# A float32 trunk whose weights are split in two parts: two rings of twelve slots instead of six tiles, wider operations, and one more seven-product row pair per block

## Chip, cores and metric

The kernel runs on one core of one Trainium2 chip. The metric is the device time of one execution in microseconds; the time before is the median of three runs. The lines of the profile come from one further execution, taken by the hardware profiler.

## The reference

A trunk of two layers works on 256 tokens of width 2048 (float32). Each layer has a token mixer (layer 0: HGRN2, layer 1: gated linear attention), a four-head attention into 256 memory tokens, an output projection, and a SwiGLU FFN. The change touches above all the FFN:

```python
hn = _rmsnorm(h, norm_ffn[layer])
gate, up = jnp.split(hn @ w_gate_up[layer], 2, axis=-1)
h = h + (jax.nn.silu(gate) * up) @ w_down[layer]
```

`w_gate_up` is 2048 x 11264 and `w_down` 5632 x 2048; the projections of the mixers (`hn @ w_in`), of the memory (`mem_n @ w_kv`) and of the output (`@ w_out`) use the same machinery for their weights.

## The kernel before

**Numbers in two parts.** TensorE multiplies in the rounded type fp32r. To keep float32 precision every operand is written as a high part (the value rounded to fp32r) and a low part (the rest), and a product is three matmuls: high x high, high x low, low x high (lines 249 to 251 in `project`, 333 to 335 in `product`). The activations are split once. The weights stream from HBM into "raw" tiles of 4 x 512 columns (four of them, line 199) and are split by `split` (line 201): ScalarE copies up to 1024 columns into the high half of a "parts" tile (line 207), and VectorE subtracts that from the raw weights into the low half (line 208). There are six parts tiles, each with two slots of 512 columns in both parts; a new one waits until TensorE has read the tile six before it.

**Plain projections.** `weights` (line 212) loads four row tiles of up to 512 columns in one transfer and splits them in two calls; `project` (line 220) multiplies them for both token halves. The FFN's down step, `w_out`, `w_in` and `w_mem_kv` go this way.

**Gate and up.** The FFN works through 11 blocks of 512 gate columns and the 512 up columns that belong to them (`up_block`, line 823). In a block, `project_halves` (line 321) goes over 8 row pairs; a pair is a 2 x 2 product of blocks (two token halves, two row tiles, gate and up). It is done in one of three ways, by a letter in `KINDS` (line 818):

- "S": seven products instead of eight, in Winograd's manner. VectorE first forms combinations of the weights in place in the raw tile, with 1024, 512 and 512 columns (lines 350 to 352); three of the four original weights and four combinations are split, in calls of 512, 1024, 1024 and 1024 columns (lines 346, 347, 353, 354).
- "O": eight products from the four original weights, two splits of 1024.
- "H": eight products too, for a pair whose activations were prepared for "S"; one combination of 512 columns (line 366) and a split of it more.

`PAIRS` (line 267) says for which kind the activations of each pair are prepared. After the eight pairs a block adds its seven sums together (lines 828 to 835), then come two down steps (`down`, line 842) on blocks that are done, each with up to two quads of four row tiles and two token halves. The work of each engine is written in program order; the order that the engines really get is fixed at build time by a scheduler that may take a later step first where an earlier one is not ready. On the chip each engine keeps to that order.

**Kinds per block:** block 0 "SHOSHOSO", blocks 1 and 2 "SHOSSOSO", blocks 3 to 10 "SSOSSOSS".

**Other tiles in the parts buffers.** The attention's keys and values for the memory (line 436) and the gate weights of layer 1 (lines 766 to 773) lie in tiles of the same six (`side`, line 193). Those of layer 1 are put away in HBM by one transfer (line 462) and fetched by one (line 767).

Of the kernel before, what the change touches and what calls it, by code (L numbers as in the profile page):

```python
# [9 lines left out]
F32 = mybir.dt.float32  # L10
F32R = mybir.dt.float32r
# [3 lines left out]
ALU = mybir.AluOpType  # L15
AX = mybir.AxisListType

P = 128
T = 256
NT = T // P  # L20
# [4 lines left out]
XA = 512  # L25
XH = 4
DFF = 5632
GR = 16
DK = 192
# [6 lines left out]
def trunk_kernel(ctx: ExitStack, tc: tile.TileContext, x, mem, norm_mix, norm_ffn, norm_mem,  # L36
                 norm_final, hgrn_w_in, hgrn_lb_logits, hgrn_onorm, gla_w_in, gla_w_gk,
                 gla_b_gk, gla_onorm, w_mem_kv, w_out, w_gate_up, w_down, c_ident, c_mask, out):
    nc = tc.nc

    const = ctx.enter_context(tc.tile_pool(name="const", bufs=1))
    wts = ctx.enter_context(tc.tile_pool(name="wts", bufs=1))
# [28 lines left out]
    h = const.tile([P, NT, D], F32, name="h")  # L71
# [106 lines left out]
    def later(*pieces):  # L178
        pending.extend(pieces)
# [12 lines left out]

    def side(shape, name):
        return wts.tile(shape, F32, tag="parts", name=name, bufs=6)

    def new_raw():
# [3 lines left out]

    def split(src, name, by=2):

        n, m = src.shape[1:]
        both = wts.tile([P, 2, 2, 512], F32R, tag="parts", name=f"parts{name}", bufs=6)
        for k in range(0, n, by):
            j = min(k + by, n)
            nc.scalar.copy(out=both[:, 0, k:j, 0:m], in_=src[:, k:j, :])  # L207
            nc.vector.tensor_tensor(out=both[:, 1, k:j, 0:m], in0=src[:, k:j, :],  # L208
                                    in1=both[:, 0, k:j, 0:m].bitcast(F32), op=ALU.subtract)
        return [(both[:, 0, k, 0:m], both[:, 1, k, 0:m]) for k in range(n)]  # L210
# [55 lines left out]

    PAIRS = "SSOSSOSB"
    HOMES = (("hq", "hq"),) * 4 + (("F", "K"), ("T", "sc"), ("Q", None), ("v", "gate"))
# [52 lines left out]
    def project_halves(forms, kinds, w, c0, c1, name):  # L321
# [15 lines left out]
        for p, kind in enumerate(kinds):  # L337
            i, raw = new_raw()

            for j, c in ((slice(0, 4, 3), c0), (slice(1, 3), c1)):  # L340
                nc.sync.dma_start(out=raw[:, j, :],
                                  in_=w[2 * p * P:(2 * p + 2) * P, c:c + 512].rearrange("(k p) c -> p k c", p=P))
            x = forms[p].get
            last = p == len(PAIRS) - 1
            if kind == "S":
                tt = nc.vector.tensor_tensor
                b00, = split(raw[:, 0:1, :], f"{i}a")
                b11, b10 = split(raw[:, 2:4, :], f"{i}b")

                tt(out=raw[:, 0:2, :], in0=raw[:, 0:4:2, :], in1=raw[:, 1:2, :].broadcast_to([P, 2, 512]), op=ALU.subtract)  # L350
                tt(out=raw[:, 2, :], in0=raw[:, 2, :], in1=raw[:, 0, :], op=ALU.add)  # L351
                tt(out=raw[:, 3, :], in0=raw[:, 3, :], in1=raw[:, 2, :], op=ALU.subtract)  # L352
                t5, t7 = split(raw[:, 0:2, :], f"{i}c")
                t6, t4 = split(raw[:, 2:4, :], f"{i}d")
                todo = {1: ("x00", b00), 2: ("x01", b10), 3: ("z", b11), 4: ("x11", t4), 5: ("s", t5), 6: ("u", t6),
                        7: ("d0", t7)}
                for b in (1, 2, 6, 7, 5, 4, 3) if last else (1, 3, 2, 5, 7, 6, 4):
                    product(b, x(todo[b][0]), todo[b][1])
            else:
                b00, b01 = split(raw[:, 0:2, :], f"{i}a")  # L360
                b11, b10 = split(raw[:, 2:4, :], f"{i}b")
                todo = [[(2, "x00", b00), (5, "x10", b01), (4, "x10", b00), (3, "d0", b01)]]
                if kind == "O":
                    todo.append([(2, "x01", b10), (5, "x11", b11), (4, "x11", b10), (3, "d1", b11)])
                else:
                    nc.vector.tensor_tensor(out=raw[:, 3, :], in0=raw[:, 3, :], in1=raw[:, 2, :], op=ALU.subtract)
                    e1, = split(raw[:, 3:4, :], f"{i}c")
# [67 lines left out]
    for l in range(2):  # L435
        kv = side([P, 2, XH * T], f"kv{l}")
        kT.append(kv[:, 0, :].rearrange("p (h t) -> p h t", t=T))
        vm.append(kv[:, 1, :].rearrange("p (m c) -> p m c", c=XA))
        ps = project(memq, range(NQ), w_mem_kv[l], 0, XA, f"mk{l}", prep=prep_mem if l == 0 else None)
# [20 lines left out]

    kv_out = away.tile([P, 2, XH * T], F32, name="kv_out")
    later(lambda: nc.scalar.dma_start(out=kv_out, in_=kv))


    def attention(l, ps, r, yq):
# [35 lines left out]
        def turn_probs(m):  # L501
            pT = st["pT", m] = work.tile([P, XH, T], F32, tag=("T", "sc")[m], name=f"pT{l}{m}")
# [260 lines left out]
    def gla(hq, r, yq):  # L763
        w = gla_w_in[0]
        half = (GR + XA) // 2
        kv = side([P, 2, XH * T], "kv")
        nc.scalar.dma_start(out=kv, in_=kv_out)
        kT[1] = kv[:, 0, :].rearrange("p (h t) -> p h t", t=T)
        vm[1] = kv[:, 1, :].rearrange("p (m c) -> p m c", c=XA)
        gk = side([P, 6, T], "gk")  # L770
        wgk = gk[:, 0:4, :]
        nc.gpsimd.memset(wgk, 0.0)
        nc.sync.dma_start(out=wgk[0:GR, :, 0:DK], in_=gla_w_gk[0].rearrange("r (h c) -> r h c", c=DK))
        psx = [project(hq, range(NQ), w, 3 * MIX + i * half, half, f"gx{i}") for i in range(2)]
        low = gk[:, 4, :].rearrange("p (t c) -> p t c", c=P)
# [3 lines left out]
        lowT = gk[:, 5, :]  # L779
        dec = {}  # L780
# [5 lines left out]
        def decay(pr):  # L786
# [3 lines left out]
            for a in range(2):  # L790
                hd = 2 * pr + a
                zp = aux_ps(f"zp{hd}")
                for j in range(2):
                    nc.tensor.matmul(zp[:, j * T:(j + 1) * T], wgk[:, hd, j * P:(j + 1) * P], lowT,
                                     start=True, stop=True)
# [21 lines left out]

    KINDS = ("SHOSHOSO", "SHOSSOSO", "SHOSSOSO", "SSOSSOSS")

# [136 lines left out]
```

## Time and profile before

| | |
|---|---|
| median of 3 runs | 2327.83 us (2327.59 to 2328.57) |
| profiled execution, its own time | 2328.0 us |
| its span, first to last instruction | 2326.2 us |
| granted TensorE clock | 0.999 |
| matmuls and transposes on TensorE | 11034 |
| split subtracts (line 208) of 1024 columns | 374, 1220 ns each |
| split copies (line 207) of 1024 columns | 374, 1050 ns each |
| data moved | 435.51 MB, 187 GB/s |

In the profile PE is TensorE's matmul, PEld its weight load, DVE VectorE, ACT ScalarE, POOL GpSimd, SP the engine whose queue issues most loads. A timeline row gives start and duration in us, engine, line, operation, output and input with their shapes, and, in brackets, how long the engine was idle before it and what released it. Names like "parts163c" are the third split of raw tile 163. Busy time of TensorE is a weak sign of how full it is, since a matmul's 0.39 us overlap with the next one; the distance between starts tells more, and the same holds for VectorE.

### The profile page before, as it was taken

Reading aid. Unit: us, or ns where it says so; the run is one execution under the profiler, and the core shown is the slowest. Engines: PE = TensorE matmul, PEld = TensorE weight load, DVE = VectorE, ACT = ScalarE, POOL = GpSimd, SP = SyncE. Lnnn points to the kernel's source line nnn. Section 1 sums busy time; section 2 is a strip of 40 time slices with the busy share of each in tenths; the row PEclk is TensorE's granted clock in tenths of the full one; section 3 lists DMA queues with packets and bytes.
Section 4 is the critical chain, followed back from the end, with each engine's and each line's share of the span. In section 5 each row is a group of like instructions: output and inputs, shape, how many; then the busy total and the mean of one; then the engine's idle time right before and its main releaser. Section 6 shows DMA issues by size and latency. Waiting matters only on the chain.

```text
span 2326.2 us, 28901 instructions
## 1 busy us (share of the span) xinstructions
PE 2303.5 (99%) x11034; PEld 1940.7 (83%) x11034; DVE 1888.0 (81%) x2262; ACT 1261.2 (54%) x1643; POOL 22.2 (1%) x39
## 2 busy tenths in 40 slices
PE   9999999999999999999999999999999999999998
PEld 7888888888887888888889999988887888888886
DVE  5565565668999999999985664557999999999995
ACT  7543535356555655555555654356555555555563
POOL 0000000000000000000000000000000000000000
PEclk9999999999999999999999999999999999999999
DMA  8554445454556555556565445455465656656563
GB/s 315 193 172 159 163 145 181 136 190 164 198 181 214 196 188 202 196 202 209 187 226 166 150 147 167 152 198 174 166 214 189 208 183 209 205 186 213 200 217 127
DMA packets 229211, 435.51 MB, mean 187 GB/s; under 512 B 10028, under 2 KB 38992, under 8 KB 228816
## 3 DMA queue, kind: packets, MB, share of 16 engines
q1 hardware_dynamic: 227776, 429.40, 54.8%
q10 hardware_dynamic: 1296, 4.26, 0.5%
q8 instruction: 86, 1.41, 0.2%
q14 instruction: 53, 0.43, 0.1%
HBM read 430.48 MB, written 3.15 MB: 186 GB/s over the span
## 4 chain that ended last, share of the span: by engine, by line
PE 63%; DVE 26%; issue 6%; ACT 4%; DMA 0%; ACTq 0%; DVEq 0%; POOLq 0%; SPq 0%
PE f_p L334 4%; PE f_p L335 4%; PE f_p L333 4%; DVE raw L350 4%; DVE parts L208 4%; PE fd L250 3%; PE fd L251 3%; PE fd L249 3%; PE wo L251 3%; PE wo L249 3%; PE wo L250 2%; DVE raw L351 2%; DVE raw L352 2%; PE slh L578 1%; PE hgate L249 1%
## 5 line engine op out<-in xcount | busy, mean ns | idle before, releaser
L208 DVE TENSOR_TENSOR parts<-raw,parts 128x1024 fp32r<-128x1024 f32 (+3 forms) x490 | 557.7, 1147 | 290.8 <-ACT parts L207 289.9
L207 ACT CAST parts<-raw 128x1024 fp32r<-128x1024 f32 (+3 forms) x490 | 476.8, 991 | 430.4 <-PE wo L251 64.4
L350 DVE TENSOR_TENSOR raw<-raw 128x1024 f32<-128x1024 f32 x118 | 143.7, 1217 | 0.2
L351 DVE TENSOR_TENSOR raw<-raw 128x512 f32<-128x512 f32 x118 | 81.6, 692 | 3.9
L352 DVE TENSOR_TENSOR raw<-raw 128x512 f32<-128x512 f32 x118 | 81.6, 692 | 3.8
L414 DVE TENSOR_TENSOR h<-fd,h 128x512 f32<-128x512 f32 x94 | 61.9, 684 | 6.2 <-PE fd L251 6.0
L831 DVE TENSOR_TENSOR e<-f_p,e 128x512 f32<-128x512 f32 x66 | 44.9, 681 | 0.0
L833 ACT ACTIVATE s<-s,rf_r 128x512 f32<-128x512 f32 x44 | 31.8, 722 | 7.0 <-DVE s L831 7.0
L562 DVE COPY_PREDICATED sch<-mask,slh 128x512 f32<-128x512 uint8 x15 | 10.8, 722 | 28.4 <-PE slh L578 28.4
L834 DVE SCALAR_TENSOR_TENSOR s<-e,rf_r,s 128x512 f32<-128x512 f32 x44 | 32.3, 741 | 0.0
L578 PEld LDWEIGHTS slh<-Q,K 128*128 128x128 f32 x240 | 29.1, 191 | 1.2
L831 DVE TENSOR_TENSOR s<-f_p,e 128x512 f32<-128x512 f32 x44 | 29.5, 683 | 0.0
L578 PE MATMUL slh<-Q,K 128*128 128x64 f32 x240 | 28.4, 271 | 0.0
L249 PE MATMUL wo<-parts,y_3h 128*128 128x512 f32 x64 | 25.9, 405 | 0.0
L249 PE MATMUL wo<-parts,y_0h 128*128 128x512 f32 x64 | 25.7, 402 | 0.0
L250 PE MATMUL fd<-parts,s_5h 128*128 128x512 f32 x64 | 25.4, 397 | 0.0
L250 PE MATMUL fd<-parts,s_7h 128*128 128x512 f32 x64 | 25.4, 396 | 0.0
L250 PE MATMUL fd<-parts,s_1h 128*128 128x512 f32 x64 | 25.3, 396 | 0.0
L249 PE MATMUL fd<-parts,s_2h 128*128 128x512 f32 x64 | 25.3, 396 | 0.0
L249 PE MATMUL fd<-parts,s_4h 128*128 128x512 f32 x64 | 25.3, 396 | 0.0
L249 PE MATMUL fd<-parts,s_6h 128*128 128x512 f32 x64 | 25.3, 396 | 0.0
L249 PE MATMUL fd<-parts,s_8h 128*128 128x512 f32 x64 | 25.3, 396 | 0.0
(5486 smaller groups left out, 7401.6 us busy)
## 6 DMA issues: line engine op xcount, KB each, us to landing
raw<-in_w_gate_up_dram SPq DMA_DIRECT2D x352, 512.0 KB, 4.0
raw<-in_w_down_dram SPq DMA_DIRECT2D x88, 1024.0 KB, 4.9
raw<-in_hgrn_w_in_dram SPq DMA_DIRECT2D x52, 1024.0 KB, 5.0
raw<-in_gla_w_in_dram SPq DMA_DIRECT2D x48, 768.0 KB, 4.3
raw<-in_w_out_dram SPq DMA_DIRECT2D x32, 1024.0 KB, 4.9
raw<-in_w_mem_kv_dram SPq DMA_DIRECT2D x15, 1024.0 KB, 8.2
raw<-in_gla_w_in_dram SPq DMA_DIRECT2D x8, 528.0 KB, 3.7
mtok<-in_mem_dram SPq DMA_DIRECT2D x4, 512.0 KB
```

Source lines behind the costliest of these rows:

```text
L207: nc.scalar.copy(out=both[:, 0, k:j, 0:m], in_=src[:, k:j, :])
L208: nc.vector.tensor_tensor(out=both[:, 1, k:j, 0:m], in0=src[:, k:j, :], in1=both[:, 0, k:j, 0:m].bitcast(F32), op=ALU.subtract)
L249: nc.tensor.matmul(acc, xh, hi[:, o:o + m], start=first, stop=False)
L250: nc.tensor.matmul(acc, xh, lo[:, o:o + m], start=False, stop=False)
L251: nc.tensor.matmul(acc, xl, hi[:, o:o + m], start=False, stop=last)
L333: nc.tensor.matmul(ps[b], xh, hi, start=first, stop=False)
L334: nc.tensor.matmul(ps[b], xh, lo, start=False, stop=False)
L335: nc.tensor.matmul(ps[b], xl, hi, start=False, stop=left[b] == 0)
L350: tt(out=raw[:, 0:2, :], in0=raw[:, 0:4:2, :], in1=raw[:, 1:2, :].broadcast_to([P, 2, 512]), op=ALU.subtract)
L351: tt(out=raw[:, 2, :], in0=raw[:, 2, :], in1=raw[:, 0, :], op=ALU.add)
L352: tt(out=raw[:, 3, :], in0=raw[:, 3, :], in1=raw[:, 2, :], op=ALU.subtract)
L578: nc.tensor.matmul(ps, st["K"][:, f, t * P:(t + 1) * P], q, start=i == 0, stop=i == len(parts) - 1)
```

## The change

The six parts tiles become two tiles, `part_h` and `part_l`, each a ring of 12 slots of 512 columns. `split` takes up to four slots at once: ScalarE copies in pieces of 1024 columns (the three original weights of "S" in one piece of 1536), but VectorE subtracts all of them in one operation, of up to 2048 columns; where the ring ends, the call is cut in two. The loads of a pair put its weights in another order in the raw tile, with three transfers instead of two, so that the three original weights that "S" splits lie side by side, and the four combinations as well; "S" becomes one split of 1536 and one of 2048 columns. The sixth pair is prepared for "S" instead of "O", and the kinds become "SHOSHHSO" (block 0), "SHOSSHSO" (1 and 2) and "SSOSSSSS" (3 to 10): seven of eight pairs in seven products. Keys, values and gate weights move to tiles of the work pool, with two transfers each way instead of one.

```diff
+    NB = 12
+    part_h = wts.tile([P, NB, 512], F32R, name="part_h")
+    part_l = wts.tile([P, NB, 512], F32R, name="part_l")
+    at = [0]
...
-        for k in range(0, n, by):
-            j = min(k + by, n)
-            nc.scalar.copy(out=both[:, 0, k:j, 0:m], in_=src[:, k:j, :])
-            nc.vector.tensor_tensor(out=both[:, 1, k:j, 0:m], in0=src[:, k:j, :],
-                                    in1=both[:, 0, k:j, 0:m].bitcast(F32), op=ALU.subtract)
+        while k < n:
+            i = at[0] % NB
+            j = min(n - k, NB - i, n if by > 1 else 1)
+            at[0] += j
+            hi, lo, s = part_h[:, i:i + j, 0:m], part_l[:, i:i + j, 0:m], src[:, k:k + j, :]
+            for c in range(0, j, by):
+                d = min(c + by, j)
+                nc.scalar.copy(out=hi[:, c:d, :], in_=s[:, c:d, :])
+            nc.vector.tensor_tensor(out=lo, in0=s, in1=hi.bitcast(F32), op=ALU.subtract)
+            pairs += [(hi[:, c, :], lo[:, c, :]) for c in range(j)]
+            k += j
...
-        return [p for k in range(0, nk, 2) for p in split(raw[:, k:k + 2, 0:n], f"{i}_{k}", 1 if i == 0 else 2)]
+        return split(raw[:, 0:nk, 0:n], 1 if i == 0 else 2)
...
-    PAIRS = "SSOSSOSB"
+    PAIRS = "SSOSSSSB"
...
+            nc.sync.dma_start(out=raw[:, 0:4:2, :],
+                              in_=w[2 * p * P:(2 * p + 2) * P, c0:c0 + 512].rearrange("(k p) c -> p k c", p=P))
+            nc.sync.dma_start(out=raw[:, 1, :], in_=hi[:, c1:c1 + 512])
+            nc.sync.dma_start(out=raw[:, 3, :], in_=lo[:, c1:c1 + 512])
...
-                b00, = split(raw[:, 0:1, :], f"{i}a")
-                b11, b10 = split(raw[:, 2:4, :], f"{i}b")
-
-                tt(out=raw[:, 0:2, :], in0=raw[:, 0:4:2, :], in1=raw[:, 1:2, :].broadcast_to([P, 2, 512]), op=ALU.subtract)
-                tt(out=raw[:, 2, :], in0=raw[:, 2, :], in1=raw[:, 0, :], op=ALU.add)
-                tt(out=raw[:, 3, :], in0=raw[:, 3, :], in1=raw[:, 2, :], op=ALU.subtract)
-                t5, t7 = split(raw[:, 0:2, :], f"{i}c")
-                t6, t4 = split(raw[:, 2:4, :], f"{i}d")
+                b00, b11, b10 = split(raw[:, 0:3, :], 3)
+
+                tt(out=raw[:, 0:4:3, :], in0=raw[:, 0:2, :], in1=raw[:, 3:4, :].broadcast_to([P, 2, 512]), op=ALU.subtract)
+                tt(out=raw[:, 1, :], in0=raw[:, 1, :], in1=raw[:, 0, :], op=ALU.add)
+                tt(out=raw[:, 2, :], in0=raw[:, 2, :], in1=raw[:, 1, :], op=ALU.subtract)
+                t5, t6, t4, t7 = split(raw)
...
-                for b in (1, 2, 6, 7, 5, 4, 3) if last else (1, 3, 2, 5, 7, 6, 4):
+                for b in (1, 2, 6, 7, 5, 4, 3) if last else (1, 3, 2, 5, 6, 4, 7):
...
-    KINDS = ("SHOSHOSO", "SHOSSOSO", "SHOSSOSO", "SSOSSOSS")
+    KINDS = ("SHOSHHSO", "SHOSSHSO", "SHOSSHSO", "SSOSSSSS")
```

More of the change, by code (lines that the diff above doesn't have):

```diff
@@ L365, in project_halves @@
                 else:
-                    nc.vector.tensor_tensor(out=raw[:, 3, :], in0=raw[:, 3, :], in1=raw[:, 2, :], op=ALU.subtract)
-                    e1, = split(raw[:, 3:4, :], f"{i}c")
+                    nc.vector.tensor_tensor(out=raw[:, 2, :], in0=raw[:, 2, :], in1=raw[:, 1, :], op=ALU.subtract)
+                    e1, = split(raw[:, 2:3, :])
                     todo.append([(2, "x01", b10), (3, "x01", b11), (7, "x11", b11), (4, "x11", e1)])
@@ L459, in trunk_kernel, with put_away @@
             nc.scalar.activation(out=vm[l][:, t, :], in_=ps[t], func=AF.Copy, scale=rm[:, t:t + 1])
-    kv_out = away.tile([P, 2, XH * T], F32, name="kv_out")
-    later(lambda: nc.scalar.dma_start(out=kv_out, in_=kv))
+    kT_out = away.tile([P, XH, T], F32, name="kT_out")
+    vm_out = away.tile([P, NT, XA], F32, name="vm_out")
+    def put_away():
+        nc.scalar.dma_start(out=kT_out, in_=kT[1])
+        nc.scalar.dma_start(out=vm_out, in_=vm[1])
+    later(put_away)
     def attention(l, ps, r, yq):
@@ L765, in gla @@
         half = (GR + XA) // 2
[L766 to L773, printed above, removed]
+        kT[1] = work.tile([P, XH, T], F32, tag="v", name="kT")
+        nc.scalar.dma_start(out=kT[1], in_=kT_out)
+        vm[1] = work.tile([P, NT, XA], F32, tag="gate", name="vm")
+        nc.scalar.dma_start(out=vm[1], in_=vm_out)
+        both = work.tile([P, 3, T], F32, tag="sc", name="gk0")
+        wgk = [both[:, 0:2, :], work.tile([P, 2, T], F32, tag="scx", name="gk1")]
+        for pr in range(2):
+            nc.gpsimd.memset(wgk[pr], 0.0)
+            nc.sync.dma_start(out=wgk[pr][0:GR, :, 0:DK], in_=gla_w_gk[0][:, 2 * pr * DK:2 * (pr + 1) * DK].rearrange(
+                "r (h c) -> r h c", c=DK))
         psx = [project(hq, range(NQ), w, 3 * MIX + i * half, half, f"gx{i}") for i in range(2)]
-        low = gk[:, 4, :].rearrange("p (t c) -> p t c", c=P)
+        low = both[:, 2, :].rearrange("p (t c) -> p t c", c=P)
         nc.gpsimd.memset(low, 0.0)
```

27 lines of the change are left out of this document (11 added, 16 removed).

## The prediction

> **What bounds the kernel now.** I read the page first: shares and slices.
>
> ```profile
> span 2326.2 us, 28901 instructions
> PE 2303.5 (99%) x11034; PEld 1940.7 (83%) x11034; DVE 1888.0 (81%) x2262; ACT 1261.2 (54%) x1643; POOL 22.2 (1%) x39
> ...
> PE   9999999999999999999999999999999999999998
> ...
> DVE  5565565668999999999985664557999999999995
> ```
>
> TensorE is busy everywhere, but VectorE is full too in two long stretches: the gate-and-up blocks of the two FFNs. Next I cut these stretches into block intervals, from one start of line 828 (the first step after a block's products) to the next, and asked for the busy time of each engine. The order of the columns is: length, PE, PEld, DVE, ACT, POOL, clock, DMA share, GB/s.
>
> ```profile
> 0.00:546.00 546.00, 540.47 (x2690) 456.38 (x2691) 327.08 (x432) 270.57 (x406) 11.33 (x18) 1.00 0.54 182
> 577.84:622.30 44.46, 43.76 (x197) 35.83 (x196) 43.16 (x50) 25.52 (x31) 0.00 (x0) 1.00 0.55 189
> 622.30:675.00 52.70, 52.70 (x238) 43.36 (x237) 50.86 (x58) 29.52 (x36) 0.00 (x0) 1.00 0.58 200
> 675.00:732.40 57.40, 56.20 (x250) 45.57 (x248) 56.76 (x65) 31.21 (x38) 0.00 (x0) 1.00 0.58 198
> 732.40:795.60 63.20, 62.97 (x279) 51.15 (x278) 62.49 (x70) 36.10 (x43) 0.00 (x0) 1.00 0.59 200
> ...
> 2183.20:2246.40 63.20, 62.97 (x279) 51.15 (x278) 62.49 (x70) 36.10 (x43) 0.00 (x0) 1.00 0.59 199
> ```
>
> The rows 675.00 to 2183.20 stand for the intervals that end with blocks 3 to 10, eight in each layer, sixteen in all. There TensorE is busy for 62.97 of 63.20 us and VectorE for 62.49: both are the bound, neither has room. Whatever the change adds to VectorE in these intervals must come out as time; what it takes from TensorE does so only if VectorE gets shorter too. Before 546 us and between the FFNs VectorE has much room, and nothing is won there by relieving it.
>
> Then the VectorE timeline inside such a block: one eight-product pair (162), one seven-product pair (163), and the start of the next.
>
> ```profile
> 956.57 1.22 DVE L208 TENSOR_TENSOR parts162a<-raw,parts162a 128x1024 fp32r<-128x1024 f32 x1
> 957.70 1.22 DVE L208 TENSOR_TENSOR parts162b<-raw,parts162b 128x1024 fp32r<-128x1024 f32 x1
> 958.84 0.68 DVE L208 TENSOR_TENSOR parts163a<-raw,parts163a 128x512 fp32r<-128x512 f32 x1
> 959.44 1.22 DVE L208 TENSOR_TENSOR parts163b<-raw,parts163b 128x1024 fp32r<-128x1024 f32 x1
> 960.57 1.22 DVE L350 TENSOR_TENSOR raw<-raw 128x1024 f32<-128x1024 f32 x1
> 961.82 0.69 DVE L351 TENSOR_TENSOR raw<-raw 128x512 f32<-128x512 f32 x1
> 962.55 0.69 DVE L352 TENSOR_TENSOR raw<-raw 128x512 f32<-128x512 f32 x1
> 963.16 1.22 DVE L208 TENSOR_TENSOR parts163c<-raw,parts163c 128x1024 fp32r<-128x1024 f32 x1
> 964.44 1.22 DVE L208 TENSOR_TENSOR parts163d<-raw,parts163d 128x1024 fp32r<-128x1024 f32 x1
> 965.58 0.69 DVE L208 TENSOR_TENSOR parts164a<-raw,parts164a 128x512 fp32r<-128x512 f32 x1
> ```
>
> Instructions overlap a little, so the price of one is the distance to the next start: 1.13 to 1.14 us for 1024 columns (956.57 to 957.70), 0.60 for 512 (958.84 to 959.44). Where an instruction needs the result of the one ahead it is 1.25 (line 350 to 351) and 0.73 (351 to 352); line 352 takes 0.61. A seven-product pair costs 965.58 - 958.84 = 6.74 us of VectorE, an eight-product pair 958.84 - 956.57 = 2.27.
>
> **The change part by part.** *TensorE.* Sixteen blocks turn one eight-product pair into a seven-product one, three matmuls less each.
>
> ```profile
> 949.01 0.39 PE L333 MATMUL f_p<-parts160a,hf_0h 128*128 128x512 f32 x1
> 949.24 0.39 PE L334 MATMUL f_p<-parts160a,hf_0h 128*128 128x512 f32 x1
> ```
>
> At 0.227 us from start to start that is 3 x 0.227 = 0.68 us per interval, 10.9 us in all: the whole gain there is to have. Blocks 0 to 2 keep their counts of products.
>
> *VectorE, width.* The columns that one pair needs stay the same; only the cuts change. From 512 to 1024 columns the price goes from 0.60 to 1.135, so 512 columns more cost 0.534, and one instruction less saves 2 x 0.60 - 1.135 = 0.067. By the same line (an estimate beyond 1024) 1536 columns cost 1.67 and 2048 cost 2.20. A seven-product pair becomes 1.67 + 1.25 + 0.73 + 0.61 + 2.20 = 6.46, against 6.74; an eight-product pair 2.20 against 2.27. Per interval: 7 x 6.46 - 6 x 6.74 = +4.78 for the seven-product pairs, 2.20 - 2 x 2.27 = -2.34 for the others. The ring of 12 cuts an operation that runs over its end: counting the positions through the program, blocks 3 to 10 have 2.9 cuts each on average (+0.19). The two down steps split four quads in an interval: 4 x (2.20 - 2 x 1.135) = -0.28, and 0.8 cuts give back 0.05. Sum: +2.40 us. The reason is plain: a seven-product pair needs 5632 columns on VectorE (splits 3584, combinations 2048), an eight-product pair 2048, and 3584 more columns at 0.534 per 512 are 3.74 us; wider operations give back only part. So VectorE's need goes from 62.5 to about 65 us while TensorE's falls to 62.3.
>
> [...]
>
> *VectorE, a new wait.* Today the last two subtracts of a seven-product pair each follow their own ScalarE copy; the copies run beside lines 351 and 352.
>
> ```profile
> 961.90 1.05 ACT L207 CAST parts163c<-raw 128x1024 fp32r<-128x1024 f32 x1 [3.14 <-DVE raw L350]
> 963.35 1.05 ACT L207 CAST parts163d<-raw 128x1024 fp32r<-128x1024 f32 x1 [0.40 <-DVE raw L352]
> 964.31 0.61 ACT L207 CAST parts164a<-raw 128x512 fp32r<-128x512 f32 x1
> ```
>
> And one subtract of an early block stood still for its copy:
>
> ```profile
> 575.81 1.23 DVE L208 TENSOR_TENSOR parts90d<-raw,parts90d 128x1024 fp32r<-128x1024 f32 x1 [1.20 <-ACT parts90d L207]
> ```
>
> A copy starts 0.11 us after the VectorE instruction that it needs (960.57 + 1.22 = 961.79, start 961.90), the next copy 0.96 after it, and takes 1.05. After the change one subtract of 2048 columns waits for both copies, and the first of them needs line 351, no longer only 350. On pair 163's clock: line 351 ends at 962.51, copies start at 962.62 and 963.58, the second ends at 964.63; VectorE would be free at 963.16. That is 1.49 us of standing still, 1.47 before the handover and 0.02 for it. Everything on VectorE queues behind it in program order: the next pair's first subtract, and with it TensorE's products. The row at 575.81 shows that such a hole of 1.20 us does occur and stays open.
>
> Whether it stays open is the question of the sum. It closes if the order written at build time puts the next pair's three-part subtract (1.67 us) into it. That needs ring slots: the next pair's first three slots are one free slot and the first two that TensorE reads from the pair before. When TensorE is starved they are free in time; when VectorE is well ahead, the ring is full and they are not. VectorE is ahead at the start of each block:
>
> ```profile
> 941.74 0.69 DVE L208 TENSOR_TENSOR parts160a<-raw,parts160a 128x512 fp32r<-128x512 f32 x1
> ```
>
> TensorE reaches the same pair at 949.01, 7.27 us later. A seven-product pair with the hole costs VectorE 6.46 + 1.49 = 7.95 and TensorE 21 x 0.227 = 4.77, so the lead shrinks by 3.2; the eight-product pair costs 2.20 against 24 x 0.227 = 5.45 and the lead grows by 3.2. Along "SSOSSSSS": 7.3, 4.1, 0.9, 4.1, 0.9, then none. So I let the holes of the first, second and fourth pair stay open (3 x 1.49 = 4.5 us) and those of the last four be filled, the very last by the steps after the block and the first split of the down step. Bounds: none open, 0; all seven open, 10.4 us. Cuts shorten a few of them, 16 of the 112 wide subtracts, and I leave that out.
>
> *Blocks 0 to 2.* Three intervals per layer. Per interval four seven-product pairs (three in block 0) take 0.28 us of VectorE less each, 1.1 in all, and one pair goes from "O" to "H", 2.20 + 2 x 0.60 = 3.40 against 2.27, 1.1 more; the need is about unchanged. Holes may open; TensorE is close behind in the rows at 577.84 and 622.30. I take 0, with -1 to +3 us for each of the six.
>
> *Loads and moved tiles.* Each pair has three loads instead of two.
>
> ```profile
> raw<-in_w_gate_up_dram SPq DMA_DIRECT2D x352, 512.0 KB, 4.0
> ```
>
> That makes 528 issues with the same bytes on a queue that does nothing else; a load lands in 4.0 us while four raw tiles are some 26 us of VectorE work. Without that cover a pair would wait up to 4 us. The keys, values and gate weights leave the split buffers: put away and fetched by two transfers each instead of one, on ScalarE's queue, ahead of projections that run long enough; and the split buffers that they held come free near the start. The row to 546.00 leaves 5.5 us of TensorE idle, so the gain is at most that; I take 0, bounds -4 and +4.
>
> **The sum.** The profiled execution took 2328.0 us (span 2326.2), 0.2 above the median of the three runs. 16 x (2.40 + 4.5) = 110; 2328 + 110 = 2438 us. A measurement of this kernel can tell some 0.2% (5 us) from no change.
>
> **The rivals.**
> *All holes filled* (22 in 100). VectorE runs without a stop, 16 x 2.40 = 38: 2366 us; if the next pair's subtract also slips between lines 350, 351 and 352, up to 0.24 per pair, 27 less. For it: VectorE has practically no gap in these blocks today. Against it: the open hole at 575.81.
> *All holes open* (12 in 100). 16 x 7 x 1.49 = 167 on top of 38: 2533 us. For it: pairs run in program order in the rows above. Against it: a starved TensorE frees the slots early.
> *TensorE sets the pace and the kernel gets faster* (4 in 100). If VectorE's need fell under 62.3 us the interval would shrink by 0.68: 2317 us. That takes 2.7 to 3 us less than the sum above, or 0.16 us less for each of the 19 wide operations of an interval than the line through 512 and 1024 columns gives. For it: nobody has timed 2048 columns in this trace. Against it: the step from 512 to 1024 columns, which leaves only 0.067 us of each operation to save.
> *No difference that can be told* (1 in 100): the same, half way.
> *The rings are guarded as two whole tiles* (3 in 100), so that the change does not act as slots: each write would wait for every earlier read, pairs would run in series, at least 4.77 us more for each of 112 pairs, over 2850 us. Against it: today the copy at 961.90 reads half of a raw tile while line 352 has yet to write another part of it; parts of a tile are told apart.
>
> **How the numbers follow.** My case, two to four holes per interval, has 58 in 100: 2328 + 38 + 16 x 1.49 x (2 to 4) is 2414 to 2461; predicted 2438. The range must take in the filled case and its lower edge, so it starts at 2355, and the high edge is five open holes and some of the bounds of blocks 0 to 2, 2490. Left out are the cases at 12, 4, 1 and 3, 20 in 100. Faster 0.04, same 0.01, slower 0.95.
>
> **What would show it.** In the changed profile: the sixteen intervals 66 to 72 us long, with VectorE's need at 65 and TensorE's busy time visibly under the length for the first time; a 2048-column subtract about 2.2 us from start to start; before it, in the early pairs of a block, idle time of about 1.5 us released by ScalarE's copy, and in late pairs the next pair's subtract ahead of it; 48 matmuls less; projections outside the FFNs unchanged. I am wrong if the intervals stay at 63 or fall, if the wide subtract is cheaper than its columns, or if VectorE is found idle for ring slots instead of for ScalarE.

## The result, and the profile after

The changed kernel takes 2500.88 us (2495.04 to 2505.14, four runs) against 2328.2 for the kernel before: 1.074 times as long, with an interval of 1.0717 to 1.0763. The sign was right; the forecast of 2438 was 63 us too low, and the range ended 11 us below the result. The profiled execution took 2505.14 us. Its page, to be set beside the shares and slices shown of before:

```profile
span 2503.4 us, 28612 instructions
...
PE 2381.4 (95%) x10986; PEld 1954.7 (78%) x10986; DVE 1924.1 (77%) x1885; ACT 1285.2 (51%) x1605; POOL 29.7 (1%) x40
...
PE   8999999999989999998999999999999999999988
...
DVE  5555555679899988988875555568998998898895
```

There are 48 matmuls less, as the diff says, and TensorE, which was full everywhere, now has gaps in the FFN blocks. VectorE has 377 instructions less and 36 us more busy time. Neither is full where both were full before. The eight block intervals of a layer (blocks 3 to 10) taken as one window each, first in the kernel before, then after; the columns are length, PE, PEld, DVE, ACT, POOL, clock, DMA share, GB/s:

```profile
675.00:1174.90 499.90, 496.82 (x2196) 403.66 (x2194) 493.98 (x548) 283.82 (x325) 0.00 (x0) 1.00 0.59 200
1746.50:2246.40 499.90, 496.98 (x2196) 403.68 (x2194) 494.00 (x548) 283.83 (x325) 0.00 (x0) 1.00 0.59 200
```

```profile
674.70:1255.80 581.10, 532.61 (x2189) 411.96 (x2189) 521.73 (x472) 296.36 (x309) 0.77 (x2) 0.96 0.51 174
1834.10:2416.50 582.40, 536.94 (x2191) 413.71 (x2190) 521.92 (x472) 296.38 (x309) 0.00 (x0) 0.95 0.51 174
```

The first window begins at 674.70 instead of 675.00: everything up to the end of block 2 of the first layer costs the same. The 16 intervals are 81.2 + 82.5 = 163.7 us longer, 10.2 each. What lies between the two windows grew from 571.6 to 578.3, what lies behind the second from 79.8 to 86.9: 13.8 more. VectorE's busy time grew by only 28 us per window; the rest, some 54, is time in which it stands. What it stands before is shown by VectorE's groups by shape in each window (count, busy us, mean ns of one, idle us ahead of them and what ended it):

```profile
L217 DVE TENSOR_TENSOR part_l<-raw,part_h 128x2048 fp32r<-128x2048 f32 x71 | 161.7, 2287 | 26.9 <-ACT part_h L216 26.3
L217 DVE TENSOR_TENSOR part_l<-raw,part_h 128x1536 fp32r<-128x1536 f32 x64 | 112.2, 1753 | 23.0 <-ACT part_h L216 23.0
...
L217 DVE TENSOR_TENSOR part_l<-raw,part_h 128x1024 fp32r<-128x1024 f32 x24 | 29.1, 1218 | 2.4 <-ACT part_h L216 2.4
L423 DVE TENSOR_TENSOR h<-fd,h 128x512 f32<-128x512 f32 x32 | 21.0, 684 | 2.3 <-PE fd L261 2.3
...
L217 DVE TENSOR_TENSOR part_l<-raw,part_h 128x2048 fp32r<-128x2048 f32 x72 | 163.8, 2287 | 30.0 <-ACT part_h L216 29.7
L217 DVE TENSOR_TENSOR part_l<-raw,part_h 128x1536 fp32r<-128x1536 f32 x63 | 110.1, 1752 | 14.7 <-ACT part_h L216 14.6
...
L423 DVE TENSOR_TENSOR h<-fd,h 128x512 f32<-128x512 f32 x32 | 21.3, 685 | 9.5 <-PE fd L261 9.5
```

Per interval that is (26.9 + 30.0)/16 = 3.6 us before the 2048-column subtracts, where the prediction had its holes, and (23.0 + 14.7)/16 = 2.4 before the 1536-column ones, where it had none. How they come about is to be seen in VectorE's timeline of one block. A row with x2 or x3 holds instructions that follow one another, under the shape of the first: 939.77 is one of 2048 columns and one of 1536, and 950.24 one of 2048 and two of 1024, a split that the end of the ring has cut.

```profile
939.77 3.96 DVE L217 TENSOR_TENSOR part_l<-raw,part_h 128x2048 fp32r<-128x2048 f32 x2 [1.42 <-ACT part_h L216]
943.76 1.23 DVE L361 TENSOR_TENSOR raw<-raw 128x1024 f32<-128x1024 f32 x1
944.90 1.75 DVE L217 TENSOR_TENSOR part_l<-raw,part_h 128x1536 fp32r<-128x1536 f32 x1
946.57 0.69 DVE L362 TENSOR_TENSOR raw<-raw 128x512 f32<-128x512 f32 x1
947.17 1.22 DVE L361 TENSOR_TENSOR raw<-raw 128x1024 f32<-128x1024 f32 x1
...
949.63 0.69 DVE L363 TENSOR_TENSOR raw<-raw 128x512 f32<-128x512 f32 x1
950.24 4.55 DVE L217 TENSOR_TENSOR part_l<-raw,part_h 128x2048 fp32r<-128x2048 f32 x3
956.19 1.76 DVE L217 TENSOR_TENSOR part_l<-raw,part_h 128x1536 fp32r<-128x1536 f32 x1 [1.40 <-ACT part_h L216]
957.99 1.23 DVE L361 TENSOR_TENSOR raw<-raw 128x1024 f32<-128x1024 f32 x1
```

and in ScalarE's and TensorE's of the same place:

```profile
943.35 1.49 ACT L216 CAST part_h<-raw 128x1536 fp32r<-128x1536 f32 x1 [2.23 <-PE f_p L345]
...
954.69 1.47 ACT L216 CAST part_h<-raw 128x1536 fp32r<-128x1536 f32 x1 [2.72 <-PE f_p L345]
```

```profile
950.12 0.73 PE L343 MATMUL f_p<-part_h,hf_4h 128*128 128x512 f32 x2 [1.00 <-ACT part_h L216]
952.58 0.80 PE L344 MATMUL f_p<-part_l,hf_4h 128*128 128x512 f32 x1 [1.72 <-DVE part_l L217]
953.17 0.63 PE L345 MATMUL f_p<-part_h,hf_4l 128*128 128x512 f32 x1
953.60 0.63 PE L344 MATMUL f_p<-part_l,hf_4h 128*128 128x512 f32 x1
```

The 1.42 at 939.77 is the forecast hole (1.49 was worked out). The 1.40 at 956.19 is another: the copy of 1536 columns is one instruction that needs three free slots, and the last of them comes free only when TensorE has read it, for the pair two before (a matmul of line 345, PE f_p L345, ends the copy's wait of 2.72). TensorE is late because it waited itself, 1.00 and 1.72 us, for the one wide copy and the one wide subtract; and from 953.17 on it runs at 0.43 us per matmul (953.17 to 953.60) instead of 0.227, with a granted clock of 0.50 from 952.00 to 955.40.

### The profile page after: what moved, and what is told of

It is laid out like the page before. It is cut to its first block, busy times and chain, and to the rows that moved or that the text cites. A ratio compares the mean times of both kernels' runs of the same rounds, so it can differ in the third digit from the quotient of the medians.

```text
span 2503.4 us, 28612 instructions
## 1 busy us (share of the span) xinstructions
PE 2381.4 (95%) x10986; PEld 1954.7 (78%) x10986; DVE 1924.1 (77%) x1885; ACT 1285.2 (51%) x1605; POOL 29.7 (1%) x40
## 5 line engine op out<-in xcount | busy, mean ns | idle before, releaser
L216 ACT CAST part_h<-raw 128x1024 fp32r<-128x1024 f32 (+4 forms) x1048 | 1042.0, 1023 | 1065.9 <-PE f_p L345 255.9
L217 DVE TENSOR_TENSOR part_l<-raw,part_h 128x2048 fp32r<-128x2048 f32 (+3 forms) x649 | 1172.6, 1824 | 395.0 <-ACT part_h L216 390.7
L344 PE MATMUL f_p<-part_l,hf_4h 128*128 128x512 f32 x156 | 70.4, 452 | 21.4 <-DVE part_l L217 21.4
L344 PE MATMUL f_p<-part_l,hf_6hl 128*128 128x512 f32 x154 | 70.9, 460 | 18.6 <-DVE part_l L217 18.1
L344 PE MATMUL f_p<-part_l,hf_7h 128*128 128x512 f32 x160 | 68.5, 428 | 11.5 <-DVE part_l L217 11.3
L343 PE MATMUL f_p<-part_h,hf_6hl 128*128 128x512 f32 x154 | 54.3, 411 | 18.6 <-ACT part_h L216 18.6
L344 PE MATMUL f_p<-part_l,hf_2h 128*128 128x512 f32 x176 | 68.7, 390 | 0.0
L345 PE MATMUL f_p<-part_h,hf_6hl 128*128 128x512 f32 x154 | 68.6, 445 | 0.0
L343 PE MATMUL f_p<-part_h,hf_2h 128*128 128x512 f32 x176 | 67.8, 393 | 0.7 <-ACT part_h L216 0.7
L345 PE MATMUL f_p<-part_h,hf_2l 128*128 128x512 f32 x176 | 68.3, 390 | 0.0
L345 PE MATMUL f_p<-part_h,hf_4l 128*128 128x512 f32 x156 | 68.2, 437 | 0.0
L345 PE MATMUL f_p<-part_h,hf_7l 128*128 128x512 f32 x160 | 66.5, 416 | 0.0
L345 PE MATMUL f_p<-part_h,hf_5l 128*128 128x512 f32 x160 | 64.2, 402 | 0.0
L345 PE MATMUL f_p<-part_h,hf_1l 128*128 128x512 f32 x160 | 62.9, 393 | 0.0
```

The costliest lines, as they stand in the source:

```text
L216: nc.scalar.copy(out=hi[:, c:d, :], in_=s[:, c:d, :])
L217: nc.vector.tensor_tensor(out=lo, in0=s, in1=hi.bitcast(F32), op=ALU.subtract)
L343: nc.tensor.matmul(ps[b], xh, hi, start=first, stop=False)
L344: nc.tensor.matmul(ps[b], xh, lo, start=False, stop=False)
L345: nc.tensor.matmul(ps[b], xl, hi, start=False, stop=left[b] == 0)
```

## The experiments

Each kernel is timed beside the kernel before (medians of 2328.5 to 2329.2). Ratios are to that one.

**Rings and seven pairs, taken apart.** e1 is the changed kernel with the old counts of products:

```diff
-    PAIRS = "SSOSSSSB"
+    PAIRS = "SSOSSOSB"
...
-    KINDS = ("SHOSHHSO", "SHOSSHSO", "SHOSSHSO", "SSOSSSSS")
+    KINDS = ("SHOSHOSO", "SHOSSOSO", "SHOSSOSO", "SSOSSOSS")
```

> The changed kernel with the kinds of before (six of eight pairs in seven products from block 3, sixth pair prepared for O): rings, loads and wide operations alone. Theory A (the 172 us are the extra pair's columns on VectorE plus holes before the 2048-column subtract): VectorE's need per interval falls to about 60.6 us, but holes of 1.4 us open in two or three pairs; interval 63 to 65 us, 2330 to 2365 us. Theory B (only the count of seven-product pairs matters, the wide operations are harmless or good): the interval stays TensorE's 63.0, 2320 to 2330 us.

Measured: 2409.21 us, 1.0346 [1.0331, 1.0362]. That is outside both ranges: VectorE's need is 61.1 us per interval, about as expected, but the idle time beside it is 6.2. So the rings and wide operations alone, with no matmul saved and no column added, cost 81 us. The idle time in the window of its first layer:

```profile
L217 DVE TENSOR_TENSOR part_l<-raw,part_h 128x2048 fp32r<-128x2048 f32 x76 | 173.5, 2288 | 41.2 <-ACT part_h L216 41.2
L217 DVE TENSOR_TENSOR part_l<-raw,part_h 128x1536 fp32r<-128x1536 f32 x55 | 96.0, 1752 | 4.3 <-ACT part_h L216 4.3
```

The window is 540.4 us long, 40.5 more than before, and 41.2 of idle time stand ahead of the 2048-column subtracts. In the second layer the window is 36.9 longer, with 21.6 ahead of 2048 columns and 10.1 ahead of 1536.

e2 is the other half: the kernel before with the new counts.

```diff
-    PAIRS = "SSOSSOSB"
+    PAIRS = "SSOSSSSB"
...
-    KINDS = ("SHOSHOSO", "SHOSSOSO", "SHOSSOSO", "SSOSSOSS")
+    KINDS = ("SHOSHHSO", "SHOSSHSO", "SHOSSHSO", "SSOSSSSS")
```

> The kernel of before with the kinds of after (seven of eight pairs): the count alone, with six tiles and operations of 1024 columns. Theory A: one pair 6.74 instead of 2.27 on VectorE, +4.5 less the small room of today, interval 66.5 to 67.5 us, 2385 to 2400 us, clock 1.00. Theory B: as slow as the changed kernel or slower, 2490 to 2530 us. Theory C (a starved TensorE loses its clock, and that is the rest): clock under 0.99 here too and over 2410 us.

Measured: 2440.85 us, 1.0482 [1.0464, 1.0499]. The seventh pair alone costs 112 us with the old buffers. No theory had this: it is slower than A, faster than B, and the clock of 0.998 speaks against C. VectorE's need is 66.4 us per interval, as worked out; what was not expected is 2.1 us of idle time in each interval and some 15 us outside them. In the window of eight intervals VectorE is busy for 531 of 548 us, TensorE has 40 us of room:

```profile
680.50:1228.80 548.30, 508.75 (x2177) 397.70 (x2177) 531.28 (x590) 300.49 (x341) 0.00 (x0) 1.00 0.54 182
```

**The 2048-column subtract.** e3 splits the four combinations in two operations, as before, and keeps all else of the change; e4 does so with the old counts.

```diff
-                t5, t6, t4, t7 = split(raw)
+                t5, t6 = split(raw[:, 0:2, :])
+                t4, t7 = split(raw[:, 2:4, :])
```

> The changed kernel with the four combinations split by two calls of 1024 columns instead of one of 2048; rings, seven pairs and all other wide operations stay. Theory A: the holes before the wide subtract go (about 3 us per interval and what follows from them), the need stays at about 66 us: interval 66 to 69 us, 2375 to 2425 us. Theory B: no change from the changed kernel, 2490 to 2510 us.

> Six pairs and the combinations split by two calls: rings and the harmless wide operations alone. Theory A: VectorE's need about 61 us without holes, the interval is TensorE's 63.0: 2322 to 2330 us, the same as before or a trace faster. Theory B: the same as e1.

Measured: e3 2418.84 us, 1.0387 [1.0371, 1.0402]; e4 2346.0, 1.0074 [1.0059, 1.0089]. The one instruction per pair is worth 82 us with seven pairs and 63 with six. e3 is in A's range; e4 is 16 us over A's and far from e1. In e3's first window (541.7 us, 39.4 less than after) the idle time ahead of both widths went:

```profile
L217 DVE TENSOR_TENSOR part_l<-raw,part_h 128x1536 fp32r<-128x1536 f32 x52 | 91.2, 1753 | 9.1 <-ACT part_h L216 8.4
...
L217 DVE TENSOR_TENSOR part_l<-raw,part_h 128x2048 fp32r<-128x2048 f32 x29 | 66.2, 2282 | 1.7 <-ACT part_h L216 1.7
```

26.9 - 1.7 before 2048 columns and 23.0 - 9.1 before 1536 make 39.1, about the difference of the window (what else changed nearly cancels: 2.4 to 7.1 before 1024 columns against 4.5 less busy time). So the holes before 1536 columns go in good part with those before 2048. But these don't make them alone: over both windows e1 has 62.8 us before 2048 columns and only 14.4 before 1536, the changed kernel 56.9 and 37.7. The seventh pair has its part in it.

**Is the ring full?** e5 gives the changed kernel 14 slots instead of 12, in place of the fourth raw tile.

```diff
-        return i, wts.tile([P, 4, 512], F32, tag="raw", name=f"raw{i}", bufs=4)
+        return i, wts.tile([P, 4, 512], F32, tag="raw", name=f"raw{i}", bufs=3)
...
-    NB = 12
+    NB = 14
```

> The changed kernel with rings of 14 slots instead of 12 (two seven-product pairs, no operation of theirs cut), paid for by three raw tiles instead of four. Theory A (part of the holes is a ring that is full: VectorE waits for a copy that waits for TensorE): holes before 1536-column subtracts, 2.4 us per interval now, shrink by half or more, and cuts go: 2440 to 2475 us. Theory D (the ring's size hardly matters; the holes come from the copies that follow the combinations): 2485 to 2505 us. Slower than 2505 would mean that the fourth raw tile was needed.

Measured: 2432.59 us, 1.0445 [1.0429, 1.046]: 68 us less than after. That is better than A's range, since both kinds of hole shrink: to 13.3 us (2048) and 8.7 (1536) in the first window. So room in the ring is what much of the idle time lacked, even at the cost of a raw tile. With 14 slots a pair's operations are no longer cut either; at 3.7 cuts per interval and 0.067 us each, an estimate from the rows of before, that is only some 4 us of the 68.

**TensorE's clock.** e6 adds matmuls with zeros, eight to each of the last four seven-product pairs in blocks 3 to 10, where TensorE waits: 512 in all, over 116 us of TensorE work at 0.227 us.

```diff
+    zero = wts.tile([P, P], F32R, name="zero")
+    nc.vector.memset(zero.bitcast(F32), 0.0)
...
+        def filler(b, left_factor):
+            nc.tensor.matmul(ps[b], left_factor[0], zero.unsqueeze(1).broadcast_to([P, 4, P]), start=False, stop=False)
...
-                for b in (1, 2, 6, 7, 5, 4, 3) if last else (1, 3, 2, 5, 6, 4, 7):
+                for n, b in enumerate((1, 2, 6, 7, 5, 4, 3) if last else (1, 3, 2, 5, 6, 4, 7)):
+                    if n == 3 and kinds[5] == "S" and p > 3:
+                        for _ in range(8):
+                            filler(b, x("x00"))
```

> The changed kernel with eight matmuls on a tile of zeros, 1.8 us, put between the third and the fourth product of the fifth to eighth pair in blocks 3 to 10, where TensorE stands idle (512 in all, they add nothing to the sums). Theory C (the half clock after TensorE's idle stretches costs time, since slots come free late): the clock goes from 0.976 to over 0.99 and the time falls to 2465 to 2490 us although 512 matmuls are added. Theory A without C (the half clock falls on time that TensorE has anyway): the clock rises, the time stays at 2495 to 2510 us or goes up by what the fillers delay.

Measured: 2473.86 us, 1.062 [1.0602, 1.0638]: 27 us faster than after, with more work. The mean clock rises from 0.976 to 0.997. As theory C had it, half clock costs time. In the first window the idle time ahead of 1536 columns is halved, that ahead of 2048 hardly changes (23.0 and 26.9 after):

```profile
L219 DVE TENSOR_TENSOR part_l<-raw,part_h 128x2048 fp32r<-128x2048 f32 x73 | 166.3, 2287 | 24.7 <-ACT part_h L218 24.7
L219 DVE TENSOR_TENSOR part_l<-raw,part_h 128x1536 fp32r<-128x1536 f32 x64 | 112.1, 1753 | 10.8 <-ACT part_h L218 10.4
```

This tells the two kinds apart: the forecast holes hardly depend on TensorE's clock, the others do, by way of the time at which TensorE frees slots.

**Which halves of the combinations.** e7 is e4 with the two halves cut otherwise, so that the first copy needs line 361 alone:

```diff
-                t5, t6 = split(raw[:, 0:2, :])
-                t4, t7 = split(raw[:, 2:4, :])
+                t5, t7 = split(raw[:, 0:4:3, :])
+                t6, t4 = split(raw[:, 1:3, :])
...
-                for b in (1, 2, 6, 7, 5, 4, 3) if last else (1, 3, 2, 5, 6, 4, 7):
+                for b in (1, 2, 6, 7, 5, 4, 3) if last else (1, 3, 2, 5, 7, 6, 4):
```

> Rings with six pairs and two calls of 1024 columns for the combinations (2346 us), but the first of them takes the two that the 1024-column combination leaves final (line 361), as the kernel before does, instead of waiting for line 362. If the remaining 17 us over the kernel before come from holes at these subtracts, which moved 0.7 us later: 2326 to 2334 us. If they come from the ring, the loads or the other wide operations: 2340 to 2348 us.

Measured: 2351.23 us, 1.0099 [1.0084, 1.0114], no better than e4's 2346.0 and a little over both ranges. The order of the halves isn't what e4 still loses.

**Filling the hole by hand.** e8 is the changed kernel with the next pair's load and first split, and this pair's first three products, written ahead of the split of the combinations.

```diff
+        def load(p):
             i, raw = new_raw()
...
+            ahead[p] = raw, split(raw[:, 0:3, :], 3) if kinds[p] == "S" else split(raw)
...
+                if not last:
+                    load(p + 1)
+                todo = {1: ("x00", b00), 2: ("x01", b10), 3: ("z", b11)}
+                order = (1, 2, 6, 7, 5, 4, 3) if last else (1, 3, 2, 5, 6, 4, 7)
+                for n, b in enumerate(order):
+                    if n == (2 if last else 3):
+                        t5, t6, t4, t7 = split(raw)
```

> The changed kernel with the program order of the pairs changed: the next pair's loads and first split stand ahead of the split of the combinations, and the first three products ahead of it too, so that the hole has work in it by construction; widths, ring and count stay. Theory A (holes are a matter of what stands in the order behind the last combination): holes at the 2048-column subtracts fall from 3.5 us per interval to under 1, time 2400 to 2450 us, near e3. Theory E (a subtract over 2048 columns delays TensorE by itself, whatever fills VectorE): 2480 to 2510 us.

Measured: 2443.01 us, 1.0489 [1.0473, 1.0505], 58 us less than after and in A's range. The 2048-column holes nearly close (5.7 us in the first window against 26.9); the 1536-column ones stay (17.0). But blocks 1 and 2 lose some 11 us in the first layer and 16 in the second (108 and 113 us against 97 in the kernel before). So the wide hole can be filled, and part of the gain is lost elsewhere.

**Narrow operations in the rings.** e9 keeps the two rings, the three loads, the moved keys, values and gates and the wide operations outside the seven-product pairs, but cuts all splits of these pairs as before and has the old counts; e13 is the same with the new counts.

```diff
-                b00, b11, b10 = split(raw[:, 0:3, :], 3)
+                b00, = split(raw[:, 0:1, :])
+                b11, b10 = split(raw[:, 1:3, :])
...
-                t5, t6, t4, t7 = split(raw)
+                t5, t6 = split(raw[:, 0:2, :])
+                t4, t7 = split(raw[:, 2:4, :])
```

> Rings of 12, six pairs, and the seven-product pairs split in calls of 512, 1024, 1024 and 1024 columns as in the kernel before; only plain projections and eight-product pairs keep one operation of 2048. If the 17 us that e4 is over the kernel before come from the one split of 1536 columns: 2326 to 2334 us. If they come from the ring, the loads or the wide operations elsewhere: 2340 to 2350 us.

> The changed kernel with the seven-product pairs split in calls of 512, 1024, 1024 and 1024 columns, 12 slots, four raw tiles: the count of seven-product pairs alone, in rings (against e9, 2328.6 us, with six). If the extra pair's columns on VectorE are the floor: need about 4.1 us per interval over e9's, less the room that TensorE leaves, interval 65.5 to 66.5 us, 2375 to 2400 us, under e3 (2418.8) by what the split of 1536 columns costs. If the narrow operations cost as much as the wide ones save: 2415 to 2445 us, as e3 or e2.

Measured: e9 2328.6 us, 1.000 [0.9991, 1.001]; e13 2397.03, 1.0294 [1.0277, 1.0311]. Their first windows, e9 and then e13 (its bounds are not exact block starts):

```profile
673.70:1176.30 502.60, 497.96 (x2206) 405.42 (x2204) 489.10 (x524) 290.34 (x347) 0.77 (x2) 1.00 0.59 198
```

```profile
676.00:1210.00 534.00, 508.82 (x2175) 400.31 (x2173) 519.31 (x574) 307.57 (x361) 0.78 (x2) 0.99 0.55 187
```

The bounds of e13's row reach beyond its eight blocks; from 675.2 to 1203.3, its block starts, they take 528.1 us, 66.0 per interval, in the range of the first theory. And e9 shows that the 17 us of e4 come from the split of 1536 columns: rings, loads and moved tiles cost nothing. With that the 172 us come apart, one step at a time: e9 2328.6; the seventh pair, +68 (e13); its first split in one operation of 1536, +22 (e3); the combinations in one of 2048, +82 (after). With six pairs the last two steps are +17 and +63, so the prices depend on one another. The seventh pair costs 44 us less here than in e2, and the trace of e13 shows one reason. Lines 362 to 364 there are the three combinations:

```profile
929.42 1.22 DVE L362 TENSOR_TENSOR raw<-raw 128x1024 f32<-128x1024 f32 x1
930.56 1.22 DVE L217 TENSOR_TENSOR part_l<-raw,part_h 128x1024 fp32r<-128x1024 f32 x1
931.69 0.69 DVE L363 TENSOR_TENSOR raw<-raw 128x512 f32<-128x512 f32 x1
932.29 0.69 DVE L217 TENSOR_TENSOR part_l<-raw,part_h 128x512 fp32r<-128x512 f32 x1
932.90 0.69 DVE L364 TENSOR_TENSOR raw<-raw 128x512 f32<-128x512 f32 x1
```

Subtracts of the pair's own first split and of others stand between the dependent combinations, so these cost 1.14 and 0.60 us from start to start instead of 1.25 and 0.73. That is up to 0.24 us per pair, 16 x 7 x 0.24 = 27 of the 44; the other 17 are not accounted for.

**More slots with fewer columns.** e10 is e4 with 14 slots and three raw tiles, e11 is e3 with them, e12 is e9 with them (the edit is e5's).

> e4 (six pairs, combinations in two calls) with rings of 14 slots and three raw tiles. If VectorE's holes in e4 (2.3 us per interval) are a full ring: they shrink under 1 us and the interval becomes TensorE's: 2320 to 2332 us, at the kernel before or a little faster. If not: 2340 to 2350 us.

> Seven pairs with both remedies at once: combinations in two calls, rings of 14 slots. VectorE's need (64 to 65 us per interval) should be what is left: 2328 + 16 x 2.5 to 3.5 = 2368 to 2390 us. Well under 2365 us would mean that the extra pair's columns are not the floor; over 2400 us that yet another wait is left.

> e9 with rings of 14 slots: the pairs of the kernel before in rings with room. If room in the ring is what the kernel before lacks, 2318 to 2326 us and a version faster than both; if TensorE is the floor already, 2326 to 2332 us.

Measured: e10 2334.85 us, 1.0026 [1.0017, 1.0035]; e11 2416.7, 1.0378 [1.0363, 1.0394]; e12 2323.69 (2321.68 to 2325.86, ten runs), 0.9979 [0.9969, 0.9988]. e10 lies between its two ranges: room in the ring takes 11 of e4's 17 us, and VectorE's idle time falls from 2.3 to 1.8 us per interval, not under 1. e11 missed: it is hardly faster than e3 (2418.84). With three raw tiles ScalarE stands before loads. From its waits (us in total, times, longest):

```profile
ACT part_h L216 <- DMA raw<-in_w_gate_up_dram: 109.2, 52, 5.1
ACT part_h L216 <- DMA raw<-in_w_down_dram: 101.7, 57, 4.8
```

But in e5 ScalarE waits as long for the same loads (107.3 and 108.3 us) and the kernel gains 68, and in e12 (130.7 and 75.4) it is the fastest of all. So these waits don't explain e11, and why two slots more bring it only 2 us stays open. e12 is faster than both kernels, by 0.2% against the one before: little, but none of its ten runs is as slow as the fastest of the other. That is in the range of its first theory. Its page shows TensorE busy for all but 21 of 2322 us, and VectorE with 43 us less than before (1888.0):

```profile
span 2322.3 us, 28993 instructions
...
PE 2301.7 (99%) x11034; PEld 1940.8 (84%) x11034; DVE 1845.0 (79%) x2050; ACT 1281.5 (55%) x1710; POOL 37.3 (2%) x40
```

e9, with 1853.8 us of VectorE, has most of the 43 too and gains nothing by it, so VectorE's busy time isn't what e12 gains by.

## Why the prediction came out too low

Against the profiled executions the kernel lost 2503.4 - 2326.2 = 177 us, where the sum had 110. VectorE's need below is the length of an interval less all its idle time, as a mean over the 16 intervals.

| us | predicted | measured |
|---|---|---|
| VectorE's need, per interval | +2.40 | +3.48 (61.75 to 65.23) |
| idle before 2048 columns | +4.5 | +3.56 |
| idle before 1536 columns | 0 | +2.36 |
| idle before line 423 (waits for TensorE) | 0 | +0.74 |
| other idle, less what before had | 0 | +0.09 |
| 16 intervals | 110 | 164 |
| all else | 0 | +13.5 |

Of the 67 us that were missed, 38 stand before 1536 columns, 17 are VectorE's need, 12 stand before line 423 and 15 are in the last two rows; against them the idle time before 2048 columns is 15 us less than forecast.

*What was right.* The bound: VectorE's columns are the floor of the intervals, and the matmuls saved bring nothing (e2: TensorE has 40 us of room in 548). The price of width: 1.67 us from start to start for 1536 columns (944.90 to 946.57), and in this timeline 2.20 for 2048:

```profile
908.58 2.29 DVE L217 TENSOR_TENSOR part_l<-raw,part_h 128x2048 fp32r<-128x2048 f32 x1
910.78 1.28 DVE L149 TENSOR_TENSOR s_5l<-tp_s_5h,s_5h 128x512 fp32r<-128x512 f32 x2
```

These are the values read off the line through 512 and 1024. The durations are 0.08 to 0.09 us longer than these distances (1752 and 2287 ns). The hole: its cause and its size came as worked out, and e1, e3 and e4 show that it is the wide operation that makes it. But there are fewer of them than forecast. Of the 40 idle stretches over 0.3 us before 2048 columns in the two windows, 26 follow copies that waited for line 362, as in the prediction; they are 1.34 to 1.42 us long (against 1.49) and make 36.7 us, 2.3 per interval instead of 4.5. In blocks 3 to 10 they open at the first pair in 9 of 16 blocks, at the fourth in 10, at the second in one, and in 4 at the sixth, where the prediction had none: VectorE's lead decides it only in part. Of the other 14, 13 with 18.4 us follow copies that waited for TensorE's products (line 345), that is, for slots. So it is luck that the row for 2048 columns comes near its forecast. Blocks 0 to 2 of the first layer, loads and moved tiles: nothing, as taken (e9).

*The step that failed* is the sentence that a starved TensorE frees the slots in time. It frees them late. In the place shown, the wide copy and the wide subtract hand TensorE its input in one piece, so it waits, and then has the products of two pairs ahead of it while the next split needs three of their slots at once. Of the 37.7 us before 1536 columns some 26 follow such copies that waited for line 345; with the 18.4 before 2048 columns that makes 45 us, 2.8 per interval, which the sum had at nothing. e5 (two slots more: -68 us) shows that room is lacking where the wide subtract is; where it isn't, two more bring 2 to 11 us (e3 to e11, e9 to e12, e4 to e10). The prediction's own sign of being wrong, VectorE idle for ring slots, came true by way of ScalarE's copy. And the starved TensorE lost clock here, 0.976 on average against 0.999 before, which the sum did not have at all. Four windows of 3.4 us around the place above, after the change:

```profile
945.20:948.60 3.40, 3.38 (x15) 2.38 (x14) 3.40 (x4) 1.05 (x1) 0.00 (x0) 1.00 0.41 158
948.60:952.00 3.40, 1.26 (x4) 0.39 (x3) 3.37 (x4) 2.94 (x3) 0.00 (x0) 0.99 0.00 0
952.00:955.40 3.40, 2.82 (x7) 2.24 (x8) 2.79 (x3) 0.71 (x1) 0.00 (x0) 0.50 0.48 114
955.40:958.80 3.40, 3.40 (x10) 2.63 (x9) 2.57 (x2) 0.76 (x1) 0.00 (x0) 0.50 1.04 396
```

One stretch in which TensorE is busy for 1.26 of 3.40 us, and the next 6.8 us are granted at 0.50. By its mean clock of 0.976 some 2 x 0.024 x 2503 = 120 us of this run passed at half clock, an estimate; the clock records of its trace add up to 121 us at 0.50. e6 takes nearly all of it away (mean clock 0.997) and wins 27 us, its own matmuls paid: that share of the miss is shown. The two pairs whose combinations are interleaved from 943.76 to 950.24 suggest how the order written at build time may add to it: VectorE finishes the combinations of both before it starts the wide subtract of the first, and TensorE runs dry from 948.6 on. What this order costs by itself stays open, since e8 changed it and lost elsewhere.

*The need* was 1.08 us too small. One part shows: line 361 overwrites raw[:, 0], which the 1536-column subtract just ahead still reads, and so starts 1.80 us after it (956.19 to 957.99; median 1.79 over the 57 places where VectorE stands for less than 0.3 us between the two) instead of 1.67. At seven pairs that is at most 0.9 us per interval, some of it counted as idle; in the kernel before the subtract ahead of line 350 read other parts of the tile, and line 350 started 1.13 us after it (959.44 to 960.57), as after any 1024 columns. It was to be seen in the diff. The rest of the 1.08 is not traced.

*All else*, 13.5 us, lies between the two windows and behind the second (6.7 and 7.1, less 0.3 ahead of the first). The prediction had 0 with bounds of +3 us for each interval of blocks 0 to 2; the last stretch, behind block 10, it did not consider.

*The rivals.* With all seven holes open it would have been 2533, nearer to the result than the forecast, but not for its reason: 1.6 holes of that kind per interval were open, not seven. Holes all filled, a TensorE that sets the pace, and rings guarded as whole tiles fell: the intervals are 72.7 us long, TensorE has room, and e9 runs at the old time with the same rings. The range was too narrow at the top, since it let none of the open holes act back on TensorE.

## What to carry to other kernels

Merging two operations saved 0.067 us here and made the merged one wait for the last of its inputs, some 1.4 us where nothing filled the hole: count the producers of a wide operation before its overhead. Where two engines are both full, price a trade in the units of the one that receives the work (3584 columns for three matmuls), and where the result overloads one, add that the starved one frees shared buffers late (2.8 us per interval here) and may lose its clock (0.976 here against 0.999). Keep the operations narrow, and try whether memory does more in the shared ring than in the load buffers: e12 is that, and the only version that beat the kernel before, by 5 us.

## What the runs showed of the hardware

The clock fell to 0.50 though TensorE never stood for long: the waits that begin in the window 948.60 to 952.00 are the 1.00 and 1.72 us of the rows above, and it was busy for 37% of that window. In this run the clock falls 26 times, each time for 3.41 or 6.83 us (the last, at the end of the span, apart), and TensorE is busy for between 14 and 57% of the 3.41 us ahead of each fall. A low share alone does not decide it: from 1095.32 to 1098.73 TensorE was busy for 1.69 us, 50%, and the clock of the next 3.42 us is 1.00. What decides it the runs do not show. And in these rows VectorE charges for an overwrite about what it charges for a result that the next instruction needs: 1.80 against 1.67 us, 0.13 more, beside 1.25 against 1.135 in the kernel before.
